# A transformer kernel on one core: both feature parts past the high weights in one 512-column matmul for half of the expert scores and the up projection of the MLP, and routing with its results innermost

## The chip, the cores and the metric

The kernel runs on one core of a Trainium2 chip. The metric is the time of one execution on the device in microseconds (us). One execution was also recorded by the hardware profiler; all rows below are of that one.

## The reference, cut to what matters

256 tokens of width 1024 go through two layers with a PEER feed-forward (after a retention mixer, then after a gated mixer), then through a block of local attention and convolution, cross-attention to a memory, and a squared-ReLU MLP. The changed parts are these:

```python
# PEER, per token: 8 heads, product keys, top 16 of 128 x 128 experts
s_top, i_top = lax.top_k(scores, 16)                       # 2 x 128 scores per head
cand = s_top[..., 0, :, None] + s_top[..., 1, None, :]     # 256 sums per head
best, pos = lax.top_k(cand, 16)
expert_idx = take(i_top0 * 128 + i_top1, pos); gates = softmax(best)
out = sum_k gelu(expert_u[idx_k] . h) * gate_k * expert_v[idx_k]
# MLP
a = relu(h @ w_up); y = (a * a) @ w_down
```

The kernel computes the scores of all 16384 experts as a dense product and multiplies by a gate that is zero for those not chosen.

## The kernel before, in words

**Products in two parts.** Every fp32 operand is split into a high part (rounded to the format of TensorE) and a low part (the rest). A product of weights and features is three matmuls: w_hi·x_hi, w_hi·x_lo, w_lo·x_hi (`mm3`, L340 to L342). A *unit* is 128x1024 weights, 512 KB: 8 chunks of 128 rows, each multiplied into 256 tokens, so 24 matmuls of 256 columns, accumulated in one half of a PSUM bank. Two units (a *pair*) share a bank.

**The split of the weights.** ScalarE (ACT) copies the high part (L293), then VectorE (DVE) or, for units marked in the plan, GpSimd (POOL) subtracts it from the raw weights for the low part (L295). In the first 64 expert units every fourth unit (i % 4 == 3) is on POOL. `get` takes a unit and first issues the split of the unit three ahead (there are three split buffers; in the MLP there are five more). All engines run their own instructions strictly in the order in which this Python code issues them.

**Expert scores (`u_units`, L966).** Each PEER layer has 128 units; the result of a pair is put through Gelu by ACT from PSUM into `S` (L974). The first 64 units (`u_units(S1, 62)`) are run while DVE does the routing; `tick` issues some of its tasks after each unit, so that the rest of the queue is spread over the units left. The second 64 run with the gates, then the `pv` units multiply the gated scores by the value rows (`V`, L1007 to L1009; these matmuls have 512 columns).

**Routing tasks (`top`, `routing_rest`).** 32 tasks `top` find the 16 best of 128 (five DVE instructions: MAX8, its index, replace, MAX8, index). Then for each of two blocks of 128 tokens: `cand` (two adds, 256 sums per head), eight `pick` (again `top`, on 256 columns), `prep`, `exp`, and twice over `eq`, `eq`, `mul`, `tree`, which turn the position of each result into an expert index by comparing it with 0 to 15, multiplying by the 16 candidates and adding them up; then `gates`, `flip` (transposes on TensorE, PE) and `land`.

**MLP up (L1864 on).** 32 units in pairs. A pair's ReLU is done by ACT from PSUM (L1872), its square by DVE (L1874), and the square is split in two by ACT (L393) and DVE (L394).

```python
for n in range(0, 32, 2):
    ...
    nc.scalar.activation(t, pt, AF.Relu)
    nc.vector.tensor_mul(r, t, t)
    self.split_to(ab[:, 0, n:n + 2], ab[:, 1, n:n + 2], r)
```

Of the kernel before, what the change touches and what calls it, by code (L numbers as in the profile page):

```python
# [157 lines left out]
class Net:  # L158
# [185 lines left out]
    def f1(self, ps, s, hs, start=True, stop=True, mid=None, half=None, **kw):  # L344
# [18 lines left out]
    def f2(self, pss, hs, tag, after=None, qs=range(4)):  # L363
        mm = self.nc.tensor.matmul
        for q in qs:
            s = self.get(tag)
            w = s.rearrange("p s (c m) -> p s c m", c=2)
            for tb in range(2):
                tt = slice(tb * P, tb * P + P)
                for c in range(2):  # L370
                    hi, lo = hs[2 * q + c]
# [13 lines left out]
    def acc_tile(self, name):  # L385
        return self.p_ps.tile([P, 512], F32, tag="acc", name=name, bufs=4)

    def accs(self, name):
        t = [self.acc_tile(name) for _ in range(4)]
        return [t[n % 4][:, (n // 4) * T:(n // 4) * T + T] for n in range(KC)]  # L390
# [3 lines left out]
        self.nc.vector.tensor_sub(lo, src, hi.bitcast(F32))  # L394

    def split_scaled(self, his, srcs, gs):
        for (hi, lo), src, g in zip(his, srcs, gs):
            self.nc.scalar.activation(hi, src, AF.Copy, scale=g)  # L398
        for (hi, lo), src, g in zip(his, srcs, gs):
# [147 lines left out]
    def run(self):  # L547
# [6 lines left out]
        self.p_ps = self.keep("pps", bufs=2, space=PSUM)  # L554
        self.p_d = self.keep("pd", space=DRAM)
        self.ident = c.tile([P, P], F32, name="ident")
        self.iota = c.tile([P, TOPK], F32, name="iota")
        self.vecs = c.tile([P, _off], F32, name="vecs")
        self.ones = c.tile([P, P], F32, name="ones")
        self.eps = c.tile([P, 1], F32, name="eps")  # L560
# [69 lines left out]
            st[0] = self.ms_root(ps, KC)  # L630

        def first():
            nc.vector.tensor_copy(self.iota, iota[:, :TOPK])
# [293 lines left out]
    def peer(self, l):  # L927
# [219 lines left out]
    def routing_rest(self, pr):  # L1147
        nc = self.nc
        H = 8
        sh = [P, H, TOPK, TOPK]  # L1150
        add = self.tasks.append

        def block(tb):
# [3 lines left out]
            r = {}  # L1157

            def cand(k):
                if k == 0:  # L1160
                    r["cand"] = pr.tile(sh, F32, tag="cand", name="cand", bufs=2)
                    r["best"] = pr.tile([P, H, TOPK], F32, tag="best", name="best")
                    r["pos"] = pr.tile([P, H, TOPK], U32, tag="pos", name="pos")
                hh = slice(4 * k, 4 * k + 4)
                s4 = [P, 4, TOPK, TOPK]
                nc.vector.tensor_tensor(r["cand"][:, hh], v4[:, hh, 0, :, None].to_broadcast(s4),
                                        v4[:, hh, 1, None, :].to_broadcast(s4), op=ALU.add)

            def pick(h):
                self.top(pr, r["cand"][:, h].rearrange("p a b -> p (a b)"), r["best"][:, h], r["pos"][:, h], T)  # L1170

            def prep():
                best = r["best"]
                top = r["top"] = pr.tile([P, H, TOPK], F32, tag="top", name="top")
                nc.vector.tensor_tensor(top, best, best[:, :, 0:1].to_broadcast([P, H, TOPK]), op=ALU.subtract)
                ab = pr.tile([P, 2, H, TOPK], U32, tag="ab", name="ab")
                nc.vector.tensor_scalar(ab[:, 0], r["pos"], 4, None, op0=ALU.logical_shift_right)
                nc.vector.tensor_scalar(ab[:, 1], r["pos"], 15, None, op0=ALU.bitwise_and)
                r["abf"] = pr.tile([P, 2, H, TOPK], F32, tag="abf", name="abf")
                nc.vector.tensor_copy(r["abf"], ab)  # L1180
                r["idb"] = pr.tile([P, 16, TOPK], BF16, tag="idb", name="idb")
                nc.vector.tensor_copy(r["idb"], idx)
# [5 lines left out]
            def eq(s_, k):  # L1188
                if k == 0:
                    r["eq"] = pr.tile(sh, BF16, tag="eq", name="eq", bufs=2)  # L1190
                hh = slice(4 * k, 4 * k + 4)
                s4 = [P, 4, TOPK, TOPK]
                nc.vector.tensor_tensor(r["eq"][:, hh], r["abf"][:, s_, hh, :, None].to_broadcast(s4),
                                        self.iota[:, None, None, :].to_broadcast(s4), op=ALU.is_equal)

            def mul(s_):
                i4 = r["idb"].rearrange("p (h s) k -> p h s k", s=2)
                nc.vector.tensor_tensor(r["eq"], r["eq"], i4[:, :, s_, None, :].to_broadcast(sh), op=ALU.mult)

            def tree(s_):  # L1200
                e = r["eq"]
                t = pr.tile([P, H, TOPK, 8], BF16, tag="tree", name="tree")
                nc.vector.tensor_tensor(t, e[:, :, :, 0:8], e[:, :, :, 8:16], op=ALU.add)
                nc.vector.tensor_tensor(t[:, :, :, 0:4], t[:, :, :, 0:4], t[:, :, :, 4:8], op=ALU.add)
                nc.vector.tensor_reduce(r["ent"][:, s_], t[:, :, :, 0:4], axis=AX.X, op=ALU.add)

            def gates():
                top = r["top"]
# [23 lines left out]
                add(lambda k=k: cand(k))  # L1232
            for h in range(H):
                add(lambda h=h: pick(h))
            add(prep)
            add(exp)
            for s_ in range(2):
                for k in range(2):
                    add(lambda s_=s_, k=k: eq(s_, k))
                add(lambda s_=s_: mul(s_))  # L1240
                add(lambda s_=s_: tree(s_))
            add(gates)
# [591 lines left out]
    def mlp(self):  # L1834
# [27 lines left out]
        self.pipe([lambda: None, total, recip, square]  # L1862
                  + [lambda k=k: turn(k % 2, k // 2) for k in range(4)])
        for n in range(0, 32, 2):  # L1864
            pt = self.mm_tile("pu").rearrange("p (j t) -> p j t", j=2)
            if n == 0:
                self.f1_pair([pt[:, 0], pt[:, 1]], "mlp_u", hs, True)
            for j in range(2 if n else 0):
                self.f1(pt[:, j], self.get("mlp_u"), hs)
            self.tick()  # L1870
            t = pa.tile([P, 2, T], F32, tag="t", name="t", bufs=2)
            nc.scalar.activation(t, pt, AF.Relu)  # L1872
            r = pa.tile([P, 2, T], F32, tag="r", name="r", bufs=2)
            nc.vector.tensor_mul(r, t, t)  # L1874
            self.split_to(ab[:, 0, n:n + 2], ab[:, 1, n:n + 2], r)
        abs_ = [(ab[:, 0, c], ab[:, 1, c]) for c in range(32)]
        self.warm(AF.Sqrt)
        ss = pa.tile([P, 2, 4], F32, name="ss")
# [48 lines left out]
```

## Time and profile before

| | us |
|---|---|
| median of 3 runs | 2541.93 (2540.96 to 2544.15) |
| the profiled execution | 2541.58 |
| its span in the trace | 2539.8 |

The span is what the trace shows; 1.8 us of the execution lie around it. "Busy" of an engine is the time in which it ran something. PE is busy for 2478.1 us of the span, DVE for 1873.1, ACT for 1259.6, POOL for 213.0.

### The profile page before, as it was taken

How to read it: one execution, taken by the hardware profiler on the slowest of the kernel's cores; microseconds unless marked ns; L12 is line 12 of the kernel's file. 1: busy time of each engine (PE TensorE's matmuls, PEld its weight loads, DVE VectorE, ACT ScalarE, POOL GpSimd, SP SyncE). 2: the span in 40 equal slices, each digit the busy share in tenths (PEclk: the TensorE clock that was granted, in tenths of full speed). 3: DMA queues.
4: the chain of work that ended last, by engine and by line, in shares of the span. 5: the costliest groups of instructions: out<-in, count | busy, mean ns of one | idle time of the engine just before them, and what ended most of it. 6: DMA issues, size and time to landing. Idle time of an engine off the chain costs nothing.

```text
span 2539.8 us, 42924 instructions
## 1 busy us (share of the span) xinstructions
PE 2478.1 (98%) x17066; PEld 2279.8 (90%) x17066; DVE 1873.1 (74%) x2974; ACT 1259.6 (50%) x1788; POOL 213.0 (8%) x155
## 2 busy tenths in 40 slices
PE   8999999999999999999999999999999999889998
PEld 7989999999988888788999999999888888889986
DVE  7767788888868778865877888888675555785654
ACT  4345544444444455556455444444445445565643
POOL 0000112200001000001121222000100000101000
PEclk8999999999999999999999999999999999999999
DMA  8685555555569888866665555555786665444553
GB/s 308 229 288 182 185 163 184 183 184 195 196 214 302 292 308 306 291 216 213 202 219 175 165 187 184 192 187 196 258 267 203 215 191 166 151 150 146 174 191 125
DMA packets 145193, 532.42 MB, mean 210 GB/s; under 512 B 16208, under 2 KB 16464, under 8 KB 144096
## 3 DMA queue, kind: packets, MB, share of 16 engines
q1 hardware_dynamic: 131616, 477.82, 57.0%
q0 software_dynamic: 12656, 49.62, 5.6%
q8 instruction: 134, 2.20, 0.3%
q10 hardware_dynamic: 720, 2.24, 0.2%
q14 instruction: 67, 0.55, 0.1%
HBM read 507.46 MB, written 22.16 MB: 209 GB/s over the span
## 4 chain that ended last, share of the span: by engine, by line
PE 79%; DVE 8%; DMA 6%; ACT 4%; issue 2%; POOL 0%; SPq 0%; ACTq 0%; DVEq 0%
PE pu L340 11%; PE pu L342 11%; PE pu L341 11%; PE V L1008 7%; PE V L1007 7%; PE V L1009 7%; DVE split L295 3%; ACT split L293 2%; PE g L1278 2%; DMA raw<-in_pv 2%; PE pq L341 1%; PE pq L342 1%; PE pq L340 1%; PE po L341 1%; PE po L342 1%
## 5 line engine op out<-in xcount | busy, mean ns | idle before, releaser
L295 DVE TENSOR_TENSOR split<-raw,split 128x1024 fp32r<-128x1024 f32 x756 | 935.4, 1241 | 548.8 <-ACT split L293 547.2
L293 ACT ACTIVATE split<-raw 128x1024 fp32r<-128x1024 f32 x808 | 851.5, 1058 | 700.6 <-PE V L1009 214.6
L340 PE MATMUL pu<-h,split 128*128 128x256 f32 x2496 | 713.7, 286 | 0.1
L342 PE MATMUL pu<-h,split 128*128 128x256 f32 x2496 | 706.4, 283 | 6.9 <-DVE split L295 6.4
L341 PE MATMUL pu<-h,split 128*128 128x256 f32 x2496 | 705.9, 283 | 0.5 <-DVE h L400 0.5
L342 PEld LDWEIGHTS pu<-h,split 128*128 128x128 f32 x2496 | 478.0, 191 | 8.4 <-DVE split L295 7.6
L341 PEld LDWEIGHTS pu<-h,split 128*128 128x128 f32 x2496 | 478.3, 192 | 0.7 <-DVE h L400 0.7
L340 PEld LDWEIGHTS pu<-h,split 128*128 128x128 f32 x2496 | 477.9, 191 | 0.6 <-ACT u L1445 0.3
L1008 PE MATMUL V<-split,a_sp 128*128 128x512 f32 x1024 | 400.8, 391 | 5.6 <-DVE split L295 5.6
L1007 PE MATMUL V<-split,a_sp 128*128 128x512 f32 x1024 | 401.5, 392 | 0.0
L1009 PE MATMUL V<-split,a_sp 128*128 128x512 f32 x1024 | 400.9, 391 | 0.0
L1008 PEld LDWEIGHTS V<-split,a_sp 128*128 128x128 f32 x1024 | 192.7, 188 | 48.1 <-DVE split L295 6.3
L1009 PEld LDWEIGHTS V<-split,a_sp 128*128 128x128 f32 x1024 | 192.7, 188 | 42.8
L1007 PEld LDWEIGHTS V<-split,a_sp 128*128 128x128 f32 x1024 | 192.6, 188 | 41.5
L974 ACT ACTIVATE S<-pu 128x512 f32<-128x512 f32 x128 | 76.5, 598 | 238.0 <-PE pu L342 238.0
L295 POOL TENSOR_TENSOR split<-raw,split 128x1024 fp32r<-128x1024 f32 x52 | 134.1, 2579 | 527.6 <-ACT split L293 516.7
L300 DVE SCALAR_TENSOR_TENSOR raw<-raw,cact 128x1024 f32<-128x1024 f32 x92 | 111.7, 1217 | 6.9 <-DMA raw<-in_ada 5.6
L340 PE MATMUL pq<-h,split 128*128 128x256 f32 x320 | 94.2, 295 | 1.5 <-ACT h L398 1.4
L341 PE MATMUL pq<-h,split 128*128 128x256 f32 x320 | 91.6, 286 | 0.7 <-DVE h L400 0.3
L342 PE MATMUL pq<-h,split 128*128 128x256 f32 x320 | 91.1, 285 | 0.6 <-DVE split L295 0.6
L1271 DVE TENSOR_TENSOR og<-og,g 128x1024 f16<-128x1024 f16 x128 | 88.0, 687 | 2.2
L394 DVE TENSOR_TENSOR a_sp<-S,a_sp 128x512 fp32r<-128x512 f32 x128 | 87.4, 684 | 1.0 <-ACT a_sp L393 0.9
(396 smaller groups left out, 3736.6 us busy)
## 6 DMA issues: line engine op xcount, KB each, us to landing
raw<-in_pu SPq DMA_DIRECT2D x256, 512.0 KB, 3.5
raw<-in_pv SPq DMA_DIRECT2D x256, 512.0 KB, 4.5
raw<-in_ada SPq DMA_DIRECT2D x92, 512.0 KB, 4.7
raw<-in_pq SPq DMA_DIRECT2D x32, 512.0 KB, 4.1
d_g<-stage POOLq DMA_DIRECT2D x32, 512.0 KB, 3.6
g<-d_g POOLq DMA_DIRECT2D x16, 1024.0 KB, 10.4
raw<-in_mlp_u SPq DMA_DIRECT2D x32, 512.0 KB, 3.9
raw<-in_mlp_d SPq DMA_DIRECT2D x32, 512.0 KB, 3.5
```

The source lines that it names most:

```text
L293: nc.scalar.activation(s[:, 0], r, AF.Copy)
L295: eng.tensor_sub(s[:, 1], r, s[:, 0].bitcast(F32))
L300: nc.vector.scalar_tensor_tensor(r, r, 1.0, self.cact, op0=ALU.mult, op1=ALU.mult, accum_out=self.mod[l][:, o:o + 1])
L340: mm(ps, w_hi, x_hi, start=start, stop=False, **kw)
L341: mm(ps, w_hi, x_lo, start=False, stop=False, **kw)
L342: mm(ps, w_lo, x_hi, start=False, stop=stop, **kw)
L394: self.nc.vector.tensor_sub(lo, src, hi.bitcast(F32))
L974: nc.scalar.activation(S[:, i - 1:i + 1], pt, AF.Gelu_apprx_tanh)
L1007: nc.tensor.matmul(o, hi, ww[:, 0], start=i == 0, stop=False)
L1008: nc.tensor.matmul(o, hi, ww[:, 1], start=False, stop=False)
L1009: nc.tensor.matmul(o, lo, ww[:, 0], start=False, stop=en)
L1271: nc.vector.tensor_tensor(og[:, k], og[:, 1], pairs(g3[:, k, b * GT:b * GT + GT]), op=ALU.mult)
```

## The change

**Wide units.** `f1_wide` does a chunk in two matmuls: w_hi against x_hi and x_lo side by side (512 columns: a third view `hs[c][2]` of the feature tile spans both), and w_lo·x_hi (256 columns) added onto the first half. A unit's result is then two halves of one bank, a pair takes two banks (`pair_tile`), and `join` adds them: ACT copies the second halves of both units out, DVE adds the first halves from PSUM. Units 4 to 63 of each PEER layer's first half (`u_first`) and pairs 1 to 15 of MLP up are wide, 150 units. Gelu runs later, on the joined result in place; so does the MLP's ReLU.

**PSUM.** `psum` closes the PSUM pool and opens it anew with another layout: before unit 4, at the end of `u_first`, behind MLP pair 0 and at the end of MLP up.

**Routing.** `cand` keeps 136 columns per head (of 16x16 sums all 16 of the first row and 8 of each other), `pick` works on these, `prep` has nine DVE instructions where it had five, and the tables of `eq` and `mul` lie with the 16 results innermost, in bf16. For that the new task `spread`, behind the fourth `pick`, casts the indices (DVE) and writes each 16 times over, in two ACT copies of 128x2048. `eq` is one instruction, `tree` four adds.

```diff
+    def f1_wide(self, ps, s, hs):
+        mm = self.nc.tensor.matmul
+        w = s.rearrange("p s (c m) -> p s c m", m=P)
+        for c in range(KC):
+            mm(ps.rearrange("p (k t) -> p k t", k=2), w[:, 0, c], hs[c][2], start=c == 0, stop=c == KC - 1,
+               skip_group_check=True)
+            mm(ps[:, :T], w[:, 1, c], hs[c][0], start=False, stop=c == KC - 1, skip_group_check=True)
+
+    def join(self, out, pt):
+        self.nc.scalar.activation(out, pt[:, :, T:], AF.Copy)
+        self.nc.vector.tensor_tensor(out, pt[:, :, :T], out, op=ALU.add)
...
+    def pair_tile(self, name):
+        return self.p_ps.tile([P, 2, 512], F32, tag="pair", name=name)
+
+    def psum(self):
+        self.shut(self.cm_ps)
+        self.cm_ps, self.p_ps = self.pool("pps", bufs=2, space=PSUM)
...
-            out += [(h[:, 0, j], h[:, 1, j]) for j in range(2)]
+            out += [(h[:, 0, j], h[:, 1, j], h[:, :, j]) for j in range(2)]
...
+        def u_first(S):
+            late = []
+            for i in range(64):
+                wide = i >= 4
+                if i == 4:
+                    self.psum()
+                if i % 2 == 0:
+                    pt = self.pair_tile("pu") if wide else self.mm_tile("pu").rearrange("p (j t) -> p j t", j=2)
+                (self.f1_wide if wide else self.f1)(pt[:, i % 2], self.get("pu"), hs)
+                if i % 2 == 1:
+                    while late:
+                        nc.scalar.activation(late[0], late.pop(), AF.Gelu_apprx_tanh)
+                    s = S[:, i - 1:i + 1]
+                    if wide:
+                        self.join(s, pt)
+                        late.append(s)
+                    else:
+                        nc.scalar.activation(s, pt, AF.Gelu_apprx_tanh)
+                self.tick(max(1, 62 - i))
+            self.drain()
+            nc.scalar.activation(late[0], late.pop(), AF.Gelu_apprx_tanh)
+            self.psum()
...
-        u_units(S1, 62)
+        u_first(S1)
...
+            def spread():
+                idb = pr.tile([P, 16, TOPK], BF16, tag="idb", name="idb")
+                nc.vector.tensor_copy(idb, idx)
+                r["idr"] = pr.tile([P, 2] + sh[1:], BF16, tag="idr", name="idr")
+                for s_ in range(2):
+                    i4 = idb.rearrange("p (h s) k -> p h s k", s=2)[:, :, s_, :, None]
+                    nc.scalar.activation(r["idr"][:, s_], i4.to_broadcast(sh), AF.Copy)
...
-                self.top(pr, r["cand"][:, h].rearrange("p a b -> p (a b)"), r["best"][:, h], r["pos"][:, h], T)
+                self.top(pr, r["cand"][:, h], r["best"][:, h], r["pos"][:, h], nw)
...
+            def eq(s_):
+                r["eq"] = pr.tile(sh, BF16, tag="eq", name="eq", bufs=2)
+                nc.vector.tensor_tensor(r["eq"], r["abf"][:, s_, :, None, :].to_broadcast(sh),
+                                        self.iota[:, None].to_broadcast(sh), op=ALU.is_equal)
             def mul(s_):
-                i4 = r["idb"].rearrange("p (h s) k -> p h s k", s=2)
-                nc.vector.tensor_tensor(r["eq"], r["eq"], i4[:, :, s_, None, :].to_broadcast(sh), op=ALU.mult)
+                nc.vector.tensor_tensor(r["eq"], r["eq"], r["idr"][:, s_], op=ALU.mult)
...
+                t = r["eq"]
+                for n in (8, 4, 2):
+                    nc.vector.tensor_tensor(t[:, :, :n], t[:, :, :n], t[:, :, n:2 * n], op=ALU.add)
+                nc.vector.tensor_tensor(r["ent"][:, s_], t[:, :, 0], t[:, :, 1], op=ALU.add)
...
                 add(lambda h=h: pick(h))
+                if h == 3:
+                    add(spread)
...
+                pt = self.pair_tile("pu")
+                for j in range(2):
+                    self.f1_wide(pt[:, j], self.get("mlp_u"), hs)
+                self.tick()
+                self.join(t, pt)
+                nc.scalar.activation(t, t, AF.Relu)
```

**Where instructions stand.** On ACT, in the first PEER layer at units 22 to 26, before: a pair's Gelu, then the high splits of two units.

```order
L974 ACTIVATE S_2653<-pu 128x512
L293 ACTIVATE split_4160<-raw_4049 128x1024
L293 ACTIVATE split_4195<-raw_4086 128x1024
L974 ACTIVATE S_2653<-pu 128x512
L293 ACTIVATE split_4232<-raw_4121 128x1024
L293 ACTIVATE split_4271<-raw_4158 128x1024
```

The same place now; L364 is the copy of `join`, L999 the late Gelu (of the pair before), L1228 the spread of the first block's indices.

```order
L364 ACTIVATE S_2653<-pu 128x512
L293 ACTIVATE split_4012<-raw_3921 128x1024
L1228 ACTIVATE idr<-idb 128x2048 x2
L293 ACTIVATE split_4038<-raw_3952 128x1024
L999 ACTIVATE S_2653<-S_2653 128x512
L364 ACTIVATE S_2653<-pu 128x512
L293 ACTIVATE split_4069<-raw_3979 128x1024
L293 ACTIVATE split_4096<-raw_4010 128x1024
```

The two spread copies now stand between the high split of unit 26 (`split_4012`) and that of unit 27 (`split_4038`), whose low part POOL takes. DVE at the same place, now: L1185 to L1190 are a `pick`, L365 is the add of `join`.

```order
L1190 MAX_INDEX pos<-best,s_4005 128x8
L295 TENSOR_TENSOR split_4012<-raw_3921,split_4012 128x1024
L1224 CAST idb<-idx_2664 128x256
L365 TENSOR_TENSOR S_2653<-pu,S_2653 128x512
L1185 MAX best<-cand 128x8
L1186 MAX_INDEX pos<-best,cand 128x8
```

The cast `idb`, which the spread reads, stands behind a pick and behind the low split of unit 26. On DVE in MLP up before, one pair:

```order
L1874 TENSOR_TENSOR r<-t 128x512
L394 TENSOR_TENSOR ab<-r,ab 128x512
L295 TENSOR_TENSOR split_24232<-raw_24122,split_24232 128x1024
L295 TENSOR_TENSOR split_24261<-raw_24160,split_24261 128x1024
```

And now:

```order
L365 TENSOR_TENSOR t<-pu,t 128x512
L1941 TENSOR_TENSOR r<-t 128x512
L415 TENSOR_TENSOR ab<-r,ab 128x512
L295 TENSOR_TENSOR split_23460<-raw_23366,split_23460 128x1024
L295 TENSOR_TENSOR split_23481<-raw_23401,split_23481 128x1024
```

The add of `join` has come ahead of each pair's square (L1941); between the two lies the ReLU, now on ACT behind the add. On PE, at the end of the first 64 units, now; what a row waits for stands in brackets.

```order
L361 MATMUL pu_5059<-h_2524,split187_5031 128x256
L340 MATMUL pu_5123<-h_2521,split188_5062 128x256 [waits DVE_49]
L341 MATMUL pu_5123<-h_2521,split188_5062 128x256
```

The first matmul behind the new PSUM layout (`pu_5123`, unit 64) waits for DVE, whose last write ahead of it is the `join` of the last wide pair.

## Rows read from the trace of the kernel before

**Rows 1.** The page: busy time of the engines, share of the span.

```profile
PE 2478.1 (98%) x17066; PEld 2279.8 (90%) x17066; DVE 1873.1 (74%) x2974; ACT 1259.6 (50%) x1788; POOL 213.0 (8%) x155
```

**Rows 2.** Windows: us, then PE, PEld, DVE, ACT, POOL, PEclk, DMA share, GB/s.

```profile
326.00:512.00 186.00, 182.79 (x1522) 182.35 (x1522) 158.85 (x387) 89.90 (x106) 42.71 (x16) 1.00 0.55 176
1396.00:1580.00 184.00, 180.79 (x1506) 180.35 (x1504) 156.56 (x377) 88.50 (x103) 42.71 (x16) 1.00 0.55 178
2345.00:2443.00 98.00, 97.52 (x811) 96.83 (x809) 67.87 (x84) 59.01 (x86) 0.60 (x1) 1.00 0.57 180
```

**Rows 3.** Waits of PE, 326 to 512 us: total us, count, longest.

```profile
PE pu L342 <- DVE split L295: 3.2, 2, 1.6
```

**Rows 4.** Timeline of PE: two matmuls 24 apart, of 256 and of 512 columns.

```profile
394.80 0.28 PE L340 MATMUL pu<-h,split 128*128 128x256 f32 x1
397.68 0.28 PE L340 MATMUL pu<-h,split 128*128 128x256 f32 x1
...
849.61 0.39 PE L1008 MATMUL V<-split,a_sp 128*128 128x512 f32 x1
855.05 0.39 PE L1008 MATMUL V<-split,a_sp 128*128 128x512 f32 x1
```

**Rows 5.** Timelines of DVE and POOL around the waits of Rows 3.

```profile
342.85 3.31 DVE L295 TENSOR_TENSOR split<-raw,split 128x1024 fp32r<-128x1024 f32 x1
...
342.70 2.38 POOL L295 TENSOR_TENSOR split<-raw,split 128x1024 fp32r<-128x1024 f32 x1 [10.01 <-ACT split L293]
```

**Rows 6.** Timeline of DVE: a low split, tops and picks.

```profile
368.08 1.20 DVE L295 TENSOR_TENSOR split<-raw,split 128x1024 fp32r<-128x1024 f32 x1
369.20 0.28 DVE L1140 MAX8 val<-s 128x8 f32<-128x128 f32 x1
370.78 0.27 DVE L1140 MAX8 val<-s 128x8 f32<-128x128 f32 x1
394.47 0.41 DVE L1140 MAX8 best<-cand 128x8 f32<-128x256 f32 x1
396.70 1.21 DVE L295 TENSOR_TENSOR split<-raw,split 128x1024 fp32r<-128x1024 f32 x1
```

**Rows 7.** Groups by line and form: count, busy us, mean ns.

```profile
L974 ACT ACTIVATE S<-pu 128x512 f32<-128x512 f32 x128 | 76.5, 598 | 238.0 <-PE pu L342 238.0
L293 ACT ACTIVATE split<-raw 128x1024 fp32r<-128x1024 f32 x808 | 851.5, 1058 | 700.6 <-PE V L1009 214.6 <-DMA raw<-in_pv 115.9 <-PE pu L342 84.2
L1198 DVE TENSOR_TENSOR eq<-eq,idb 128x2048 bf16<-128x2048 bf16 x8 | 9.7, 1218 | 0.1
L1193 DVE TENSOR_TENSOR eq<-abf,iota 128x1024 bf16<-128x1024 f32 x16 | 28.0, 1768 | 0.0
L1369 DVE TENSOR_TENSOR v<-pv,bv 128x512 f32<-128x512 f32 x12 | 7.7, 681 | 0.0
```

**Rows 8.** Operations of one stage: lowest, median, highest ns, window.

```profile
L1415 DVE SCALAR_TENSOR_TENSOR t<-wsum,vecs,bs x24: 342/345/2481, 1213.3 to 1289.2; 128x128 f32<-128x128 f32 x24
L1417 DVE SCALAR_TENSOR_TENSOR s<-psp,vecs,t x24: 482/483/488, 1213.8 to 1289.6; 128x256 f32<-128x256 f32 x24
```

**Rows 9.** Timelines of DVE, then of ACT, in MLP up.

```profile
2365.86 1.74 DVE L461 RECIPROCAL rstd<-rs 128x256 f32<-128x256 f32 x1
2414.35 0.69 DVE L1874 TENSOR_TENSOR r<-t 128x512 f32<-128x512 f32 x1 [0.96 <-ACT t L1872]
2416.69 2.36 DVE L295 TENSOR_TENSOR split<-raw,split 128x1024 fp32r<-128x1024 f32 x2 [0.26 <-ACT split L293]
2420.10 0.69 DVE L1874 TENSOR_TENSOR r<-t 128x512 f32<-128x512 f32 x1 [1.05 <-ACT t L1872]
...
2353.68 0.60 ACT L1872 ACTIVATE t<-pu 128x512 f32<-128x512 f32 x1 [0.65 <-issue]
2442.32 0.60 ACT L1872 ACTIVATE t<-pu 128x512 f32<-128x512 f32 x1 [1.78 <-PE pu L342]
```

**Rows 10.** Window at the start of the value stage, columns as in Rows 2.

```profile
750.00:765.00 15.00, 9.38 (x34) 7.34 (x33) 6.84 (x7) 3.63 (x4) 1.15 (x1) 0.78 0.73 237
```

More of the change, by code (lines that the diff above doesn't have):

```diff
@@ L370, in f2 @@
                 for c in range(2):
-                    hi, lo = hs[2 * q + c]
+                    hi, lo = hs[2 * q + c][:2]
                     first, last = q == 0 and c == 0, 2 * q + c == len(hs) - 1
@@ L396, in split_scaled @@
     def split_scaled(self, his, srcs, gs):
-        for (hi, lo), src, g in zip(his, srcs, gs):
-            self.nc.scalar.activation(hi, src, AF.Copy, scale=g)
-        for (hi, lo), src, g in zip(his, srcs, gs):
+        for h, src, g in zip(his, srcs, gs):
+            self.nc.scalar.activation(h[0], src, AF.Copy, scale=g)
+        for (hi, lo, *_), src, g in zip(his, srcs, gs):
             self.nc.vector.scalar_tensor_tensor(lo, src, g, hi.bitcast(F32), op0=ALU.mult, op1=ALU.subtract)
@@ L553, in run @@
         self.p_split = self.keep("psplit", bufs=SPLIT_BUFS)
-        self.p_ps = self.keep("pps", bufs=2, space=PSUM)
+        self.cm_ps, self.p_ps = self.pool("pps", bufs=2, space=PSUM)
+        self.ctx.callback(lambda: self.shut(self.cm_ps))
         self.p_d = self.keep("pd", space=DRAM)
         self.ident = c.tile([P, P], F32, name="ident")
-        self.iota = c.tile([P, TOPK], F32, name="iota")
+        self.iota = c.tile([P, TOPK, TOPK], BF16, name="iota")
         self.vecs = c.tile([P, _off], F32, name="vecs")
@@ L632, in first @@
         def first():
-            nc.vector.tensor_copy(self.iota, iota[:, :TOPK])
+            nc.vector.tensor_copy(self.iota, iota[:, :TOPK, None].to_broadcast([P, TOPK, TOPK]))
             nc.vector.tensor_copy(self.iota_rep, iota[:, :, None].to_broadcast([P, P, 2]))
@@ L1150, in routing_rest @@
         sh = [P, H, TOPK, TOPK]
+        h8 = TOPK // 2
+        nw = TOPK + h8 * (TOPK - 1)
         add = self.tasks.append
@@ L1160, in cand @@
                 if k == 0:
-                    r["cand"] = pr.tile(sh, F32, tag="cand", name="cand", bufs=2)
+                    r["cand"] = pr.tile([P, H, nw], F32, tag="cand", name="cand", bufs=2)
                     r["best"] = pr.tile([P, H, TOPK], F32, tag="best", name="best")
                     r["pos"] = pr.tile([P, H, TOPK], U32, tag="pos", name="pos")
+                    s3 = [P, H, TOPK]
+                    nc.vector.tensor_tensor(r["cand"][:, :, :TOPK], v4[:, :, 0, 0:1].to_broadcast(s3), v4[:, :, 1],
+                                            op=ALU.add)
                 hh = slice(4 * k, 4 * k + 4)
-                s4 = [P, 4, TOPK, TOPK]
-                nc.vector.tensor_tensor(r["cand"][:, hh], v4[:, hh, 0, :, None].to_broadcast(s4),
-                                        v4[:, hh, 1, None, :].to_broadcast(s4), op=ALU.add)
+                s4 = [P, 4, TOPK - 1, h8]
+                nc.vector.tensor_tensor(r["cand"][:, hh, TOPK:].rearrange("p h (a b) -> p h a b", b=h8),
+                                        v4[:, hh, 0, 1:, None].to_broadcast(s4),
+                                        v4[:, hh, 1, None, :h8].to_broadcast(s4), op=ALU.add)
+            def spread():
[5 more added lines that the diff above has]
+                    nc.scalar.activation(r["idr"][:, s_], i4.to_broadcast(sh), AF.Copy)
             def pick(h):
-                self.top(pr, r["cand"][:, h].rearrange("p a b -> p (a b)"), r["best"][:, h], r["pos"][:, h], T)
+                self.top(pr, r["cand"][:, h], r["best"][:, h], r["pos"][:, h], nw)
             def prep():
@@ L1175, in prep @@
                 nc.vector.tensor_tensor(top, best, best[:, :, 0:1].to_broadcast([P, H, TOPK]), op=ALU.subtract)
[L1176 to L1182, printed above, removed]
+                ab = pr.tile([P, H, TOPK], U32, tag="ab", name="ab")
+                pf = pr.tile([P, 3, H, TOPK], F32, tag="pf", name="pf")
+                r["abf"] = pr.tile([P, 2, H, TOPK], BF16, tag="abf", name="abf")
+                nc.vector.tensor_copy(pf[:, 0], r["pos"])
+                nc.vector.tensor_scalar(ab, pf[:, 0], float(h8), -float(h8), op0=ALU.max, op1=ALU.add)
+                nc.vector.tensor_scalar(ab, ab, 3, None, op0=ALU.logical_shift_right)
+                nc.vector.tensor_copy(pf[:, 1], ab)
+                nc.vector.tensor_copy(r["abf"][:, 0], pf[:, 1])
+                nc.vector.tensor_scalar(pf[:, 2], pf[:, 0], float(TOPK), -float(h8), op0=ALU.is_ge, op1=ALU.mult)
+                nc.vector.scalar_tensor_tensor(pf[:, 0], pf[:, 1], -float(h8), pf[:, 0], op0=ALU.mult, op1=ALU.add)
+                nc.vector.tensor_add(r["abf"][:, 1], pf[:, 0], pf[:, 2])
                 r["ent"] = pr.tile([P, 3, H, TOPK], F32, tag="ent", name="ent")
@@ L1186, in exp @@
                 nc.scalar.activation(r["top"], r["top"], AF.Exp)
[L1188 to L1194, printed above, removed]
+            def eq(s_):
+                r["eq"] = pr.tile(sh, BF16, tag="eq", name="eq", bufs=2)
+                nc.vector.tensor_tensor(r["eq"], r["abf"][:, s_, :, None, :].to_broadcast(sh),
+                                        self.iota[:, None].to_broadcast(sh), op=ALU.is_equal)
             def mul(s_):
-                i4 = r["idb"].rearrange("p (h s) k -> p h s k", s=2)
-                nc.vector.tensor_tensor(r["eq"], r["eq"], i4[:, :, s_, None, :].to_broadcast(sh), op=ALU.mult)
+                nc.vector.tensor_tensor(r["eq"], r["eq"], r["idr"][:, s_], op=ALU.mult)
             def tree(s_):
[L1201 to L1205, printed above, removed]
+                t = r["eq"]
+                for n in (8, 4, 2):
+                    nc.vector.tensor_tensor(t[:, :, :n], t[:, :, :n], t[:, :, n:2 * n], op=ALU.add)
+                nc.vector.tensor_tensor(r["ent"][:, s_], t[:, :, 0], t[:, :, 1], op=ALU.add)
             def gates():
@@ L1237, in block @@
             for s_ in range(2):
-                for k in range(2):
-                    add(lambda s_=s_, k=k: eq(s_, k))
+                add(lambda s_=s_: eq(s_))
                 add(lambda s_=s_: mul(s_))
@@ L1864, in mlp @@
         for n in range(0, 32, 2):
-            pt = self.mm_tile("pu").rearrange("p (j t) -> p j t", j=2)
+            t = pa.tile([P, 2, T], F32, tag="t", name="t", bufs=2)
             if n == 0:
+                pt = self.mm_tile("pu").rearrange("p (j t) -> p j t", j=2)
                 self.f1_pair([pt[:, 0], pt[:, 1]], "mlp_u", hs, True)
[L1868 to L1872, printed above, removed]
+                self.tick()
+                nc.scalar.activation(t, pt, AF.Relu)
+                self.psum()
+            else:
+                pt = self.pair_tile("pu")
+                for j in range(2):
+                    self.f1_wide(pt[:, j], self.get("mlp_u"), hs)
+                self.tick()
+                self.join(t, pt)
+                nc.scalar.activation(t, t, AF.Relu)
             r = pa.tile([P, 2, T], F32, tag="r", name="r", bufs=2)
@@ L1875, in mlp @@
             self.split_to(ab[:, 0, n:n + 2], ab[:, 1, n:n + 2], r)
+        self.psum()
         abs_ = [(ab[:, 0, c], ab[:, 1, c]) for c in range(32)]
```

## The prediction, made before the changed kernel ran

> **What bounds the kernel now.** I read the page first: PE is busy for 98% of the span [rows 1], so a change pays only if it shortens PE's work, or a wait of PE. Then the windows of the three stretches that change [rows 2]: the first 64 units of either PEER layer and MLP up. PE is busy for 182.8 of 186, 180.8 of 184 and 97.5 of 98 us. DVE, which must deliver the low half of the weights, is busy for 158.9 of 186 and 156.6 of 184 in the PEER stretches: it is the next bound, and its reserve is some 27 us in each. ACT has over half of its time free. Then the waits of PE in the first stretch [rows 3]: two of 1.6 us, both for a low split on DVE. The timelines show why [rows 5]: DVE's split began at 342.85 and took 3.31 us where one takes 1.20 [rows 6]; POOL was splitting from 342.70 to 345.08, and DVE's ended 1.08 us behind that, as if it had begun only then. So an operation with two SBUF sources on DVE and POOL's split exclude each other. Layer 2 shows the same windows, and I take its PEER stretch as equal.
>
> **The change part by part.**
>
> *Matmuls.* 24 matmuls of 256 columns take 2.88 us, 24 of 512 columns 5.44 [rows 4]: 120.0 and 226.7 ns each. The difference, 106.7, is 256 columns at the higher clock level (2.4 GHz, granted clock 1.00 in these windows [rows 2]), so each matmul has 13.3 ns beyond its columns. A chunk was 3 x 120.0 = 360 ns and becomes 226.7 + 120.0 = 346.7. A unit: 8 x 13.3 = 0.107 us less, 2.773 for 2.880. That is −6.4 us for the 60 wide units of a layer and −3.2 for the 30 of the MLP, −16.0 in all where PE is the bound. For this size a page has another figure: the Trainium skill (TensorE: Matmul & The Clock Gate, section on the wait of 56 instead of 53.3 ns) gives a matmul about 2.5 ns beyond its columns; by that, an estimate from that page, 150 units x 8 x 2.5 ns = 3.0 us would be saved in all and the total would come out some 10 us higher. The row does not agree (13.3 ns), and the sum goes by the row.
>
> *What `join` puts on DVE.* 30 adds of 128x512 per layer at 0.68 (row L1369, two SBUF sources; one of `join`'s is PSUM) are 20.4 us. On ACT the copy and the late Gelu are two of 0.60 where there was one. An add with a PSUM source was not held up by POOL: L1417 took 482 to 488 ns in all 24 cases, while L1415, all in SBUF, went to 2481 in the same stage [rows 8]. I take `join` as free of POOL; if it is not, see the rivals.
>
> *Routing on DVE.* A top on 128 columns has a pitch of 1.58 (369.20 to 370.78), a pick on 256 of 2.23 (394.47 to 396.70) [rows 6]; in proportion, one on 136 takes 1.62. 16 picks: −9.8 us a layer. `eq`: two of 128x1024 fp32 (1.77 in the mean with POOL's delays [rows 7]; 1.2 by its elements, as the split of that size [rows 6]) become one of 128x2048, all bf16, like `mul`, 1.22 (row L1198) [rows 7]. Four such a layer: −4.8 undisturbed. `cand` about −1.7, by its elements, and `prep` +2.2 per layer (four small operations more per block at 0.27, the MAX8 of [rows 6] being the nearest row); `tree` I take as equal. Sum with the joins: 20.4 − 9.8 − 4.8 − 1.7 + 2.2 = +6.3 us of DVE in a stretch that should become 6.4 shorter: of the reserve of 27 some 14 stay. The total would fit; what decides is the order.
>
> *The spread.* Two ACT copies of 128x2048. 512 columns take 0.60, 1024 take 1.06 [rows 7]: 0.46 for each 512 more, so 1.98 each, 3.8 for the two back to back. Below, if ACT were twice as fast on bf16: 1.0 each. I take 1.95, since no ACT row is faster per element. It stands on ACT between the high split of unit 26 and that of unit 27 (order, above), and waits for `idb`, which stands on DVE behind a pick and the low split of unit 26. To see what that does I walked the four queues forward on paper, instruction by instruction in program order, each with its row's duration, starting when its engine, its inputs, its buffer and (for two SBUF sources) POOL allow; done for the kernel before this gives two waits of 1.57 and unit 63 ending within 0.1 us of the trace. In the changed kernel, counted from the start of the unit loop: PE ends unit 23 at 68.7; low split 26 ends on DVE at 73.4, `idb` at 73.6; the spread runs on ACT from 73.7 to 77.5; high split 27 from 77.5 to 78.5; its low part on POOL, 2.4 us [rows 5], to 80.9. PE is through with unit 26 at 77.05. It waits 1.48 for the high and 2.22 for the low part: 3.7 us. Three units later, a low split of DVE stands behind POOL's next one: 1.7. The second block's spread lies ahead of unit 49, whose low part is DVE's: 0.9 + 0.95, and 2.7 at unit 50, again behind POOL. Together +9.9 per layer.
>
> *New layouts of PSUM.* The first wide matmul waits for the Gelu of the pair before (+0.65); the first of unit 64 for the last `join` (order, above): copy 0.60, add 0.68 and what it costs to hand over, +1.35. The rest of the walk's waits (transposes of `flip` behind `gates`, and short ones at units 35, 36, 54 and 59) come to +3.4. The two old waits go, with two short ones −3.4 in the walk of before.
>
> A layer: −6.4 − 3.4 + 9.9 + 2.0 + 3.4 = **+5.5**.
>
> *MLP up.* Here DVE's chain per pair is what counts [rows 9]. From one square (2414.35) to the next (2420.10) are 5.75 us, of which DVE idles 1.05 waiting for the ReLU; so square, high part, low part and two weight splits take 4.70. `join` (0.69 + 0.04 to hand over) and the ReLU behind it (0.60 + 0.04), on which DVE waits, add 1.37: 6.07 a pair, more than the 2 x 2.773 = 5.55 that PE needs. Pair 1 now waits for the ReLU of pair 0, 0.6, then takes 5.55, its copy 0.6, and DVE has up to half a split (0.7) ahead of its `join`: that begins 7.6 us (with 0.15 for handing over) after 2353.68. 14 pairs of 6.07 and the reciprocal of 1.74 [rows 9] follow, and the add, 0.7, for which the next stage's new layout waits: 7.6 + 85.0 + 1.7 + 0.7 = 95.0. Before, 2442.32 − 2353.68 = 88.6. **+6.4** (4 if some of these are hidden, 7 if none).
>
> *Sum.* 2541.6 (the profiled execution: span 2539.8 and 1.8 around it, 0.35 below the median) + 2 x 5.5 + 6.4 = **2559.0 us**.
>
> Bounds, per layer, from the same walk: spread copies of 1.0 each give +1.7 for +5.5; 0.5 each about 0; 0.2 each −3.6; none −6.5. `join` at 0.9 instead of 0.69: +11.6. POOL blocking nothing: −0.9. The clock: in the one window where PE stood still for 5.6 us the granted clock fell to 0.78 [rows 10]; the old waits of 1.6 left it at 1.00 [rows 2, 3]. A wait of 3.7 lies between; if the clock fell behind the spreads, 1.7 to 3.4 us each would come on top. I take none, being nearer the short waits, and keep up to 7 for the range.
>
> **The rivals.**
>
> *Faster: the spread is hidden.* If `idb` comes earlier than I have it, or the copies take below 0.3 us each, high split 27 is ready before PE ends unit 26, and the knock-on waits go. For it: DVE's sum fits with 14 us to spare, ACT is half idle. Against: the walk has DVE behind at that place, and no ACT row is that fast. A layer is then −6.5 and the total 2541.6 − 13 + 6.4 = 2535; with the MLP bound by PE also (−3), 2525.
>
> *Nothing to measure.* Half of it hidden (1.0 down to 0.5 us a copy, or DVE a few us ahead of my walk): 0 to −3 a layer and +4 to +6 in the MLP, 2540 to 2547.
>
> *Much slower: the bf16 `eq` runs at the rate of fp32*, 2.2 us instead of 1.2 (twice the 1.12 of 128x1024 between 368.08 and 369.20 [rows 6]), since both its operands are broadcast. By the walk +11.8 a layer for +5.5: 2541.6 + 23.6 + 6.4 = 2572. Row L1198, which also reads a broadcast, speaks against. Or `join` is held up by POOL: DVE's adds then slide behind every fourth split, +21 a layer by the walk, 2590. Rows L1417 speak against it. The Trainium skill (SBUF — State Buffer, Who interferes with whom) says that DVE with at most one source in SBUF is not in GpSimd's way, which is how these rows look; no run here shows `join` itself.
>
> **How the numbers follow.** As walked, 2549 to 2571: 0.50. Worse (both of the last rivals): 0.14. Hidden in half: 0.13. Hidden and faster: 0.23. Likeliest 2559. The range leaves out the lowest part of the fast case (PE-bound MLP too, under 2534) and the worst: 2534 to 2576. What this kernel's measurement can tell from no change is about 0.2%, 5 us: faster below 2537, which most of the fast case is, and slower above 2547. Faster 0.22, same 0.13, slower 0.65.
>
> **What would show each step right or wrong.** Wide units 2.77 us apart where nothing waits, and two rows per chunk of 227 and 120 ns. A gap of PE of some 3.7 us at unit 27 of each layer, its releasers ACT's split and then POOL's, with L1228 at 1.95 on ACT ahead; if the gap is missing, so is most of the +5.5. Picks at 1.62, `eq` at 1.2. L365 below 0.75 also while POOL runs. In MLP up a period of 6.07 on DVE and gaps of PE of 0.5 a pair; the first `pd` matmul released by L365. The forecast is wrong if L1228 is short or DVE is ahead at unit 24, or if PE's waits in the MLP are missing because splits five units ahead let PE run on.

## The result, and the profile after

The changed kernel takes 2559.7 us (median of 6 runs), the kernel before 2541.4: ratio 1.0082, 95% interval 1.0070 to 1.0095, which is 18 to 24 us slower. Forecast were 2559.0.

The page's first line now, to be held against [rows 1], and under it the chain of work that ended last, by engine: before, and then now.

```profile
PE 2476.5 (97%) x15866; PEld 2215.9 (87%) x15866; DVE 1885.5 (74%) x3073; ACT 1312.9 (51%) x1871; POOL 211.9 (8%) x155
PE 79%; DVE 8%; DMA 6%; ACT 4%; issue 2%; POOL 0%; SPq 0%; ACTq 0%; DVEq 0%
PE 74%; DVE 11%; DMA 6%; ACT 5%; issue 3%; POOL 0%; SPq 0%; ACTq 0%; DVEq 0%; POOLq 0%
```

1200 matmuls fewer, and PE is busy for 1.6 us less; its share of the chain went mostly to DVE. To see where the time went I measure a PEER layer's first half by ACT's eviction of the first pair and of the 33rd, the first behind the new layout. Timeline of ACT, before and then after:

```profile
332.43 0.60 ACT L974 ACTIVATE S<-pu 128x512 f32<-128x512 f32 x1 [0.91 <-PE pu L342]
521.62 0.60 ACT L974 ACTIVATE S<-pu 128x512 f32<-128x512 f32 x1 [1.81 <-PE pu L342]
```

```profile
330.47 0.60 ACT L1005 ACTIVATE S<-pu 128x512 f32<-128x512 f32 x1 [0.90 <-PE pu L342]
526.94 0.60 ACT L1019 ACTIVATE S<-pu 128x512 f32<-128x512 f32 x1 [1.82 <-PE pu L342]
```

In layer 1 189.19 us became 196.47: +7.3. In layer 2 they became 196.52. From ACT's ReLU of MLP pair 0 to the first matmul of the down projection it was 88.4 (2353.7 to 2442.1) and is 96.2 (2361.6 to 2457.8): +7.8; and in the down projection, from the start of its first matmul to that of its last of line L386 (L373 before), it was 88.8 and is 90.6: +1.8. Together 2 x 7.3 + 9.6 = 24.2. The profiled span grew by 17.6 only (2539.8 to 2557.4); the other 6.6 came out shorter in stretches that the change does not touch (between the two first halves, for one, 876.9 and 874.4 us; over all traces of this case it is 872.0 to 882.2), so I read them as this execution's and not the change's. The runs' 18 to 24 us lie between the two sums.

What PE waits for in layer 1's first half, which now ends later (326 to 528 us), and in MLP up (2350 to 2460), in place of [rows 3]:

```profile
PE pu L361 <- DVE split L295: 2.9, 2, 2.1
PE pu L361 <- POOL split L295: 2.0, 1, 2.0
PE ptr L1278 <- DVE ent L1273: 2.0, 2, 1.2
PE pu L359 <- ACT split L293: 1.7, 2, 1.0
PE pu L340 <- DVE S L365: 1.4, 1, 1.4
PE pu L359 <- ACT S L1005: 0.7, 1, 0.7
...
PE pd L386 <- DVE t L365: 6.2, 1, 6.2
```

And the place of the first spread: timelines of ACT, PE, POOL and DVE.

```profile
398.87 3.71 ACT L1228 ACTIVATE idr<-idb 128x2048 bf16<-128x2048 bf16 x2 [3.18 <-DVE idb L1224]
402.49 1.04 ACT L293 ACTIVATE split<-raw 128x1024 fp32r<-128x1024 f32 x1
403.95 0.58 ACT L364 ACTIVATE S<-pu 128x512 f32<-128x512 f32 x1
...
403.58 0.50 PE L359 MATMUL pu<-h,split 128*128 128x512 f32 x1 [1.00 <-ACT split L293]
406.07 0.39 PE L361 MATMUL pu<-h,split 128*128 128x256 f32 x1 [2.00 <-POOL split L295]
...
403.66 2.36 POOL L295 TENSOR_TENSOR split<-raw,split 128x1024 fp32r<-128x1024 f32 x1 [14.40 <-ACT split L293]
...
398.55 0.29 DVE L1224 CAST idb<-idx 128x256 bf16<-128x256 uint32 x1
404.56 0.69 DVE L365 TENSOR_TENSOR S<-pu,S 128x512 f32<-128x512 f32 x1 [5.72 <-ACT S L364]
```

The reader sees the forecast's sequence: cast, spread, high split of unit 27, its low split on POOL, and PE standing still first for the one and then for the other. The last row is what the forecast did not name: DVE does nothing for 5.72 us, for the add of `join` wants a copy that stands behind the spread on ACT.

### The profile page after: what moved, and what is told of

It is laid out like the page before. It is cut to its first block, busy times and chain, and to the rows that moved or that the text cites. A ratio compares the mean times of both kernels' runs of the same rounds, so it can differ in the third digit from the quotient of the medians.

```text
span 2557.4 us, 40704 instructions
## 1 busy us (share of the span) xinstructions
PE 2476.5 (97%) x15866; PEld 2215.9 (87%) x15866; DVE 1885.5 (74%) x3073; ACT 1312.9 (51%) x1871; POOL 211.9 (8%) x155
## 4 chain that ended last, share of the span: by engine, by line
PE 74%; DVE 11%; DMA 6%; ACT 5%; issue 3%; POOL 0%; SPq 0%; ACTq 0%; DVEq 0%; POOLq 0%
PE V L1053 7%; PE V L1052 7%; PE V L1054 7%; PE pu L359 7%; PE pu L340 6%; PE pu L341 6%; PE pu L342 6%; DVE split L295 4%; PE pu L361 3%; ACT split L293 3%; DMA raw<-in_pv 2%; PE g L1339 2%; PE pq L341 1%; PE pq L342 1%; PE pq L340 1%
## 5 line engine op out<-in xcount | busy, mean ns | idle before, releaser
L359 PE MATMUL pu<-h,split 128*128 128x512 f32 x1200 | 427.3, 400 | 6.0 <-ACT split L293 3.3
L340 PE MATMUL pu<-h,split 128*128 128x256 f32 x1296 | 373.7, 288 | 3.0 <-DVE S L365 2.8
L341 PE MATMUL pu<-h,split 128*128 128x256 f32 x1296 | 366.7, 283 | 0.5 <-DVE h L421 0.5
L342 PE MATMUL pu<-h,split 128*128 128x256 f32 x1296 | 366.6, 283 | 0.5 <-POOL split L295 0.3
L361 PE MATMUL pu<-h,split 128*128 128x256 f32 x1200 | 338.5, 282 | 11.9 <-DVE split L295 8.0
L359 PEld LDWEIGHTS pu<-h,split 128*128 128x128 f32 x1200 | 226.9, 189 | 62.7 <-ACT split L293 4.6
L340 PEld LDWEIGHTS pu<-h,split 128*128 128x128 f32 x1296 | 248.0, 191 | 4.1 <-DVE S L365 3.5
L341 PEld LDWEIGHTS pu<-h,split 128*128 128x128 f32 x1296 | 248.4, 192 | 0.8 <-DVE h L421 0.7
L342 PEld LDWEIGHTS pu<-h,split 128*128 128x128 f32 x1296 | 248.1, 191 | 1.1 <-POOL split L295 0.8
L361 PEld LDWEIGHTS pu<-h,split 128*128 128x128 f32 x1200 | 228.1, 190 | 14.2 <-DVE split L295 9.5
L1019 ACT ACTIVATE S<-pu 128x512 f32<-128x512 f32 x64 | 38.4, 599 | 129.7 <-PE pu L342 129.6
L340 PE MATMUL pq<-h,split 128*128 128x256 f32 x320 | 94.3, 295 | 1.4 <-ACT h L419 1.4
```

Source lines behind the costliest of these rows:

```text
L340: mm(ps, w_hi, x_hi, start=start, stop=False, **kw)
L341: mm(ps, w_hi, x_lo, start=False, stop=False, **kw)
L342: mm(ps, w_lo, x_hi, start=False, stop=stop, **kw)
L359: mm(ps.rearrange("p (k t) -> p k t", k=2), w[:, 0, c], hs[c][2], start=c == 0, stop=c == KC - 1, skip_group_check=True)
L361: mm(ps[:, :T], w[:, 1, c], hs[c][0], start=False, stop=c == KC - 1, skip_group_check=True)
```

## The experiments

Ratios are to the kernel before, run beside each. "Layer" is the stretch of 189.19 us measured above.

**Routing alone.** Scores (`u_units(S1, 62)`) and MLP as before.

> Only the new routing (136 candidates, spread, bf16 tables); scores and MLP as in the kernel before. Theory (order of the queues decides): the spread still stands on ACT ahead of the high splits of units 27 and 49, so two to three waits of 1.5 to 2.1 us a layer take the place of the two old ones; about +0.4 us a layer, 2542 us. Rival (DVE's load decides): DVE has some 14 us a layer less to do, the old waits go and none comes; 2535 us.

Ratio 0.9999 (0.9987 to 1.0011). Layer 189.4. Where the spreads stand PE waits 1.4, 0.2 and 1.6 us for low splits, in place of the two old waits of 1.6. As the theory has it, with two waits of that size and not three; relieving DVE of work wins nothing here while ACT is held.

**Wide units alone.** Routing and MLP as before.

> Only the wide units of the expert scores, with their PSUM layouts; routing and MLP as before, so no spread. Theory: the picks on 256 columns and the two eqs leave DVE no room for the joins, low splits come late behind POOL's (ten waits of 0.6 to 1.7 us a layer); +10 us a layer, 2561 us. Rival (the spread is all that costs): without it a layer gains 6.4 less 2.0 for the layouts; 2533 us. Rival (matmuls of 512 columns give nothing): +13 to +16 a layer.

Ratio 1.0078 (1.0064 to 1.0091). Layer 199.7: +10.5 for +10. Some 1.5 of it is the clock, which the theory leaves out: in each layer the granted clock fell once, to 0.50 for some 3.5 us, behind a wait of 2.1 at a `flip`. Waits of PE in layer 1's first half:

```profile
PE pu L361 <- DVE split L295: 8.8, 11, 1.8
PE ptr L1263 <- DVE ent L1258: 3.1, 2, 2.1
```

There is no spread here, and a layer is slower than with one: the joins do not fit in beside the old routing. The rival that only the spread costs is out; that matmuls of 512 columns give nothing would have been +13 or more.

**The MLP alone.** Scores and routing as before.

> Only the wide pairs of MLP up. Theory: the join and the ReLU stand one after the other in DVE's chain, 6.0 us a pair, and the down projection waits for the last join; +7 us, 2548 us. Rival (splits five units ahead let PE run on, PE bound): -3 us, 2538 us.

Ratio 1.0047 (1.0032 to 1.0061): 8 to 15 us. 96.2 us up to the down projection, as in the whole change, and 91.2 in place of 88.8 for that. This is on the theory's side, and more than it said.

**The spread in quarters.** Two heads behind each of the picks 4 to 7.

```diff
-                for s_ in range(2):
-                    nc.scalar.activation(r["idr"][:, s_], i4.to_broadcast(sh), AF.Copy)
+                if h >= 4:
+                    hh = slice(2 * (h - 4), 2 * (h - 4) + 2)
+                    for s_ in range(2):
+                        nc.scalar.activation(r["idr"][:, s_, hh], i4.to_broadcast([P, 2, TOPK, TOPK]), AF.Copy)
```

> The whole change, with the spread cut up: the cast where it was, then two copies of 128x512 on ACT behind each of picks 4 to 7 in place of two of 128x2048. Theory (ACT held for 3.7 us makes the high split late): the waits at units 27, 49 and 50 go, a layer is 6 us faster than before, MLP still +7; 2536 us. Rival (the joins' load on DVE and the layouts are the cause, the spread only lies there): 2556 to 2560 us, as the changed kernel.

Ratio 1.0002 (0.9993 to 1.0011). Layer 185.6 in both: −3.6, that is 10.9 less than in the whole change, though the same elements are copied. No wait for a split is left in the first halves; layer 1's, 326 to 519 us:

```profile
PE ptr L1281 <- DVE ent L1276: 1.6, 2, 0.9
PE pu L340 <- DVE S L365: 1.4, 1, 1.4
PE pu L359 <- ACT S L1005: 0.7, 1, 0.7
```

So the loss of the layers comes from the way in which the spread is issued; the rival falls. Size and place changed together, for the quarters also stand later, behind picks 4 to 7; no run separates the two. What the layers win the MLP takes.

**A short chain in the MLP.**

```diff
-                nc.scalar.activation(t, t, AF.Relu)
-            nc.vector.tensor_mul(r, t, t)
+                nc.vector.scalar_tensor_tensor(r, t, 0.0, t, op0=ALU.max, op1=ALU.mult)
```

> The whole change, but in the MLP's wide pairs ReLU and square are one operation of DVE, max(t, 0) x t, behind the join's add, so that ACT's ReLU leaves the chain. Theory (the serial chain of join and ReLU sets MLP up): 5.3 us a pair, below PE's 5.55; the wait of 6.2 for the last join falls to 1 to 2.5, some 7 us less than the changed kernel; 15 us above the kernel before, 2553 us. Rival (DVE's load, not the chain): the join's time stays, 2558 to 2560 us.

Ratio 1.0061 (1.0044 to 1.0079). 89.6 us up to the down projection for 96.2, and 88.9 for that: +1.3 over before, for +9.6. As the theory has it.

**Low weights last.**

```diff
             mm(ps.rearrange("p (k t) -> p k t", k=2), w[:, 0, c], hs[c][2], start=c == 0, stop=c == KC - 1,
                skip_group_check=True)
+        for c in range(KC):
             mm(ps[:, :T], w[:, 1, c], hs[c][0], start=False, stop=c == KC - 1, skip_group_check=True)
```

> The whole change, but each wide unit runs its eight matmuls of 512 columns first and then the eight of 256, so the low weights are wanted 1.8 us later. Theory (at the spread PE waits first for the high split, then for the low one): the waits for low splits, 5 to 7 us a layer in three or four places, lose up to 1.6 each; a layer +2 to +3 for +7.3; 2549 us. Rival (DVE behind for good, its load decides): the waits only move; 2558 to 2560 us.

Ratio 1.0085 (1.0069 to 1.0101), layer 198.2: the theory in this form was wrong. PE and DVE at the first spread:

```profile
402.98 2.12 PE L359 MATMUL pu<-h,split 128*128 128x512 f32 x8 [1.17 <-ACT split L293]
405.52 1.22 PE L362 MATMUL pu<-h,split 128*128 128x256 f32 x8 [0.42 <-POOL split L295]
...
403.97 0.69 DVE L366 TENSOR_TENSOR S<-pu,S 128x512 f32<-128x512 f32 x1 [5.73 <-ACT S L365]
```

The wait for POOL's low split fell from 2.00 to 0.42, as meant, and the time came back later: pairs 15 to 19 took 33.6 us together, where they had taken 29.5 (some 1.5 of it is a fall of the clock, which in the whole change stands at pair 13). DVE's idle stretch is the same. I formed a new theory from it: the hold of ACT is paid by DVE, which loses 5.7 us that its later work lacks; PE's wait at unit 27 is only where that first shows.

**Picks in the hold.** Three further tasks (picks) issued at the end of `spread`.

> The whole change with the spread as it is, but three picks are issued on DVE straight behind the spread's cast (later units have fewer). Theory, mended after the run with the low weights last: what is lost for good is the 5.7 us in which DVE stands at the join's add, because its copy is behind the spread on ACT. With work for DVE there, PE still waits 3 to 3.7 at the spread, but the later waits go: a layer +1 to +3 for +7.3, 2548 us. Rival (ACT's hold of the high split is the whole price): as the changed kernel, 2559 us.

Ratio 1.0058 (1.0045 to 1.0071), some 6 us less than the whole change, half of what was expected. Layer 1 took 192.0 (+2.8, inside the expectation), layer 2, the same instructions, 197.65 (+8.5). Windows of the two:

```profile
328.00:525.00 197.00, 187.35 (x1119) 164.15 (x1118) 163.57 (x429) 115.28 (x142) 41.73 (x16) 1.00 0.53 177
1398.00:1600.00 202.00, 192.34 (x1113) 167.69 (x1112) 164.57 (x429) 115.48 (x142) 40.47 (x16) 0.97 0.52 171
```

The granted clock was 1.00 in the first and 0.97 in the second, where it fell behind three of the waits. The layer of the whole change in which the clock held, its second, took 196.5. So where the clock held, the new theory's number came; that DVE's lost time is the whole price is not shown by this.

**Narrow units with the quartered spread.** Routing in quarters, scores and MLP as before.

> The new routing with the spread in quarters, all matmuls and PSUM as before. Theory: DVE is relieved and nothing holds ACT, so the two old waits go and none comes; 3.4 us less a layer, 2532 us; so nearly all that the quarters with wide units gained (3.6) is the routing's. Rival (wide units are what gains): 2539 us, as before.

Ratio 0.9964 (0.9951 to 0.9977), layer 185.4. With wide units it was 185.6: in these layers the wide units win nothing that the waits at the layouts (2.1) and the flips (1.6), shown above for the quarters and absent here, do not take again.

**Quarters, MLP as before.** The scores wide.

> The whole change with the spread in quarters, and MLP up as before. Theory: a layer 3.6 us faster, as the trace of the quarters showed, and nothing in the MLP; 2531 us, 7 below the kernel before. Rival (the quarters' equal time is chance and the MLP costs nothing): 2538 us.

Ratio 0.9960 (0.9946 to 0.9973), layer 185.6 both times. The same as the narrow one.

**No new layout behind MLP up.** The last `psum()` goes; `pd` takes `mm_tile` for the first half, `st_tile` for the second.

> The whole change, but at the end of MLP up PSUM keeps its layout and the down projection takes the four other banks; the chain of join, ReLU and square is as in the change. Theory (the chain of 6.0 us a pair is the price): DVE is as late as before, and the first values that the down projection wants are long there, so the wait of 6.2 at its start goes; but with two pair tiles PE must follow the chain, so little is won: 2556 us. Rival (the wait for the layout alone is the price, PE never follows the chain within 15 pairs): 7 to 9 us less than the changed kernel, 2551 us.

Ratio 1.0050 (1.0035 to 1.0066). 90.0 us for 96.2 up to the down projection, 88.8 for that. The wait of 6.2 is gone, and with it the lower clock behind it. The time, 2553.0, lies between the theory's and the rival's: for ten pairs PE runs ahead of the chain, as the rival has it, but from pair 11 on it follows. The first matmuls of these pairs start 6.0 us apart, each just behind the end of the `join` of two pairs before. Timeline of PE, then of DVE:

```profile
2442.39 0.50 PE L359 MATMUL pu<-h,split 128*128 128x512 f32 x1
2448.39 0.50 PE L359 MATMUL pu<-h,split 128*128 128x512 f32 x1 [0.18 <-DVE t L365]
...
2441.64 0.69 DVE L365 TENSOR_TENSOR t<-pu,t 128x512 f32<-128x512 f32 x1
2447.65 0.68 DVE L365 TENSOR_TENSOR t<-pu,t 128x512 f32<-128x512 f32 x1
```

With the short chain the same five pairs take 5.65 each, so following costs some 1.7 us. The whole change does the same from 2421.8 us on.

**All four mended.** Quarters, short chain, low weights last, no new layout behind MLP up.

> The change with the spread in quarters, the short chain in the MLP, the low weights last, and no new PSUM layout at the end of MLP up (the down projection takes the other four banks). Theory: 3.6 to 5 us less a layer than before, 2 to 3 less in the MLP; 2526 to 2529 us. Rival (wide matmuls save nothing in the end): 2538 us.

Ratio 0.9944 (0.9929 to 0.9959), 2525.1 us. Layer 185.0, 4.2 less than before, as expected; MLP up 87.5, 0.8 less and not 2 to 3. The time alone does not refute the rival, for the narrow units with the quartered spread gain most of it too; the next run does.

**And the tail.** An empty task between `gates` and `flip`, and units 62 and 63 narrow.

> The kernel with all four mended, and two more: an empty task between gates and flip, so that the transposes come a unit later, and the last pair of each first half narrow, so that the new layout waits for a Gelu and not for a join. Theory: flips save 0.9 each of 1.3, the layout 0.6 a layer; 4 us less than that kernel, 2522 us. Rival (these waits are hidden elsewhere): 2526 us.

Ratio 0.9941 (0.9929 to 0.9954), 2525.2 us. Layer 183.5, 1.5 less than without, for two layers 3 us, which the runs can't tell from the kernel above. What the wide units are worth once the waits around them are gone shows against the narrow ones with the quartered spread, run beside this kernel: 2522.3 to 2526.8 us against 2528.2 to 2533.8, some 6 us; in a layer 183.5 against 185.4. Both mended kernels beat the kernel before by 0.4 to 0.7%, and the changed one by more than 1%.

## Why the prediction was right, and where not

*The place of the loss was right.* Of the waits that the walk of the queues gave, those at the spreads, layouts and flips came. Spread copies took 1.89 to 1.91 each (1.95 forecast), 3.71 the pair. At unit 27 PE waited 1.00 + 2.00 for 1.48 + 2.22. In layer 2, where the clock held, pairs 12 and 13 (the first spread) took 14.8 us, 3.7 above two of 5.55, and pairs 23 to 25 (the second) 21.2, 4.6 above three: 3.7 and 0.9 + 0.95 + 2.7 were forecast. In layer 1 they took 16.4 and 22.7. The first wide matmul waited 0.7 (0.65), the first of unit 64 1.4 (1.35). A pick took 1.62, as forecast. `join`'s add took 0.672 to 0.695 us in all 60 cases of the two layers, 21 of them while POOL was splitting: it was not held up. The Trainium skill (SBUF — State Buffer, Who interferes with whom) states this of an operation of DVE with at most one source in SBUF, and the trace agrees. The rows from which the forecast took that `join` is free of POOL show less than it made of them: of the 24 L1417 [rows 8] only four ran beside a split of POOL. `eq` took 1.22 in the median, at the rate of L1198 [rows 7]; two of the eight, which began while POOL was splitting, took 3.4.

*Terms that were mis-sized.* The layer: +7.3 for +5.5, and the two layers came to it in different ways. Windows of layer 1 before, then of layers 1 and 2 and of two places in layer 1 now; columns as in [rows 2]:

```profile
332.43:521.62 189.19, 185.98 (x1550) 185.50 (x1549) 161.25 (x374) 89.49 (x104) 40.57 (x16) 1.00 0.55 179
330.47:526.94 196.47, 185.78 (x1070) 161.72 (x1069) 161.08 (x417) 111.92 (x138) 40.11 (x16) 0.98 0.51 172
1401.35:1597.87 196.52, 184.04 (x1071) 159.56 (x1070) 163.19 (x417) 111.91 (x139) 40.02 (x16) 1.00 0.51 172
406.00:410.00 4.00, 3.93 (x14) 3.40 (x15) 3.83 (x14) 0.94 (x2) 0.02 (x1) 0.59 0.63 192
478.00:482.00 4.00, 4.00 (x16) 3.41 (x15) 3.83 (x16) 0.00 (x0) 0.00 (x0) 0.57 0.74 238
```

In layer 1 PE's waits at the two spreads and behind them sum to 6.6 (9.9 forecast). But the granted clock, which the forecast took as holding there, fell to its lower level, 0.50, behind either spread. A fall cost some 1.5 us, a little less than the 1.7 to 3.4 of the forecast's bounds: pair 13 took 6.5 us, and 5.0 in layer 2, where the same waits left the clock at 1.00. In layer 2 PE waited 2.1 more instead, for a low split at unit 54, where the walk has a short wait; the sum there is 8.6. That both layers took 196.5 is chance. DVE's load, forecast at +6.3, stayed as it was in layer 1 and rose by 1.9 in layer 2 (161.3 us before), so the loss is not one of DVE's sum. The knock-on at unit 30 did not come (pairs 15 and 16 are 11.1 together, two undisturbed ones). Instead the flips cost more (pairs 19 and 30 were 1.1 to 1.9 too long, of which 0.3 is as before), and the term "−6.4" for the wide units was too large: where PE waited for nothing, pairs 3 to 11 took 5.65 us in the mean and not 5.55. (The Trainium skill, TensorE: Matmul & The Clock Gate, section on the wait of 56 instead of 53.3 ns, gives a matmul some 2.5 ns beyond its columns; by an estimate from that figure a pair would take 5.72, and no undisturbed stretch of the two layers does.) The MLP: +9.6 for +6.4. DVE's period was 6.00 (6.07), but the first `join` began 9.8 us behind the ReLU of pair 0 and not 7.6, as a table load of 1.28 and a root of 0.48 stood ahead of its copy on ACT; and 1.8 came on top behind the wait. Timeline of PE at the down projection:

```profile
2457.79 0.79 PE L386 MATMUL pd<-split,ab 128*128 128x512 f32 x1 [6.17 <-DVE t L365]
2458.38 0.63 PE L387 MATMUL pd<-split,ab 128*128 128x512 f32 x1
2458.81 0.63 PE L388 MATMUL pd<-split,ab 128*128 128x512 f32 x1
```

Matmuls 0.43 us apart, where [rows 4] have 0.227: behind its wait of 6.17 us PE ran at the lower of its two levels (granted clock 0.50 from 2457 to 2460 us). Here too the sum had put the clock at nothing. That the total fits to 1 us in 18 is partly chance: 17.4 was forecast for stretches that measured 24.2.

*A step that was half wrong.* "Here DVE's chain per pair is what counts." The chain of 6.0 us was there, but for ten pairs PE ran ahead of it and for the last five it followed, at some 1.7 us in all. Most of the price was the new layout, which waits for the chain's last link: 6.2, and 1.8 for the clock behind it. Taking the layout away gave back all of that; taking the lag away (short chain) left a wait of 1.4.

*A step that was incomplete.* The forecast took the lateness of unit 27's split as the price of the spread. The run with the low weights last took 1.6 us of that wait away and gained nothing. What is shown: cutting up the spread removes 10.9 us a layer (the clock's falls and the wait at unit 54 among them), hiding the first wait removes none. That DVE's idle 5.7 us carry the rest is argued from the rows, and half supported by the run with the picks; it is not shown.

*The rivals.* Neither of the slower ones came, by the rows of `eq` and `join` above. "The spread is hidden" did not happen either; the quarters show what it would have given: 185.6 a layer, −3.6, for the −6.5 forecast.

## What to carry to other kernels

A long operation on an engine with time to spare can cost more than its own length: ask what stands behind it in that engine's order, and which loaded engine has its next instruction waiting on that. Cutting it into pieces and placing them apart was worth 10.9 us a layer here. And when a PSUM pool is laid out anew, the next matmul waits for whatever still reads the old one (0.7, 1.4 and 6.2 us here): look for free banks first.

## What the runs showed of the hardware that was not expected

The wide chunk has two paces, in undisturbed stretches of one trace. Timeline of PE, nine chunks apart and eleven chunks apart:

```profile
369.91 0.40 PE L359 MATMUL pu<-h,split 128*128 128x512 f32 x1
373.09 0.40 PE L359 MATMUL pu<-h,split 128*128 128x512 f32 x1
...
417.92 0.40 PE L359 MATMUL pu<-h,split 128*128 128x512 f32 x1
421.74 0.39 PE L359 MATMUL pu<-h,split 128*128 128x512 f32 x1
```

353 ns and 347 ns a chunk, where three narrow matmuls took 360 [rows 4]. In the first, every third chunk lasts 361 ns and the two others 349 to 350. So a chunk saves 7 or 13 ns; with the low weights last a pair takes 5.59. In the two layers the pace changed only where PE had waited; what sets it was not found.
